# Sharing the scaling of the normed tiles at five layer ends between ScalarE and VectorE

## The chip, the cores and the metric

The kernel runs on one core of a Trainium2 chip. The metric is the device time of one execution in microseconds. Three runs of the kernel before took 980.38, 981.84 and 982.14 us; their median is 981.84 us. The engines are called as the profile calls them: PE (TensorE, matrix products and transposes), DVE (VectorE), ACT (ScalarE), POOL (GpSimd) and SP (SyncE, which issues the loads). Each engine works through its own list of instructions strictly in the order in which they are written, and waits by semaphores for results of the others.

## The reference

The program is a chain of four layers on 256 tokens of width 1024, all in float32: stick-breaking attention with a gated conv feed-forward part, forgetting attention with another feed-forward part, a pooling layer, and a latent (MLA) attention layer. Between any two parts stands the same step: a result is added to the residual stream `h`, `h` is normalised per token, multiplied by a gain vector, and goes into the next projection:

```python
def rmsnorm(x, g):
    xf = x.astype(jnp.float32)
    y = xf * lax.rsqrt(jnp.mean(xf * xf, axis=-1, keepdims=True) + RMS_EPS)
    return (y * g.astype(jnp.float32)).astype(x.dtype)

h = h + rmsnorm(merge_heads(o) @ sb_w_o[layer], sb_post_g[layer])   # an attention's end
f = conv_ffn(rmsnorm(h, ffn_pre_g[layer]), w_up[layer], ...)        # the next part's start
h = h + rmsnorm(f, ffn_post_g[layer])                               # a feed-forward part's end
```

The pooling layer adds its product to `x` without a norm of its own (`return x + y @ w_out`), and the MLA layer then starts with the norm of the sum.

## The kernel before

The 256 tokens are two row tiles of 128, called i = 0 and i = 1 here. Every float32 operand of a product is kept as two float32r parts, a high part (the rounded copy) and a low part (the difference), and each product is three matmuls: high by high, high by low, low by high (lines 79 to 81, and in another order lines 87, 88 and 90). ACT makes high parts (`hi_copy`, line 64) and DVE low parts (`lo_sub`, line 68), of activations and of all weights. Weights stream through a ring: SP loads a chunk of 1 MB into `raw`, and the background steps `bg_hi` and `bg_lo` put one ACT copy and one DVE subtraction of 128x1024 elements (`wh`, `wl`) into the lists of these engines, wherever the code calls them. No scheduler reorders anything: the order of the calls in the code is the order on each engine.

The step between two parts is the function `edge` (line 478). It is called five times: at the end of the first attention (E1), the first feed-forward part (E2), the second attention (E3), the second feed-forward part (E4) and the pooling layer (E5). For row tile 0, `tail0` ends the sums in two PSUM banks (`accO`, `accD` or `accP`; columns 0 to 511 and 512 to 1023, called H0 and H1 here). Then, with `post_add` (E1 to E4):

- `half(n)` takes a bank into the post norm. ACT squares it and sums the squares (`square`, line 383, an ACTIVATE and the reading of its accumulator), and DVE multiplies it by the post gain into `y` (lines 394 and 397). The two read the same bank and never at once: for H0 of row tile 1 DVE goes first and ACT waits for it, for all others ACT goes first.
- `fin` makes the factor r of the post norm on POOL by `rstd_of` (three small operations on 128x1: lines 346, 348 and, with the power, 349) and updates `h` by two DVE operations (line 402).
- `norm_r` sums the squares of `h` on ACT (line 383, two halves), lets DVE make one waiting `wl` (`bg_lo`), and makes the factor of the pre norm on POOL.
- `scaled` (line 370) makes the normed tile `a` = h times r times g, by two DVE operations of 128x512, H0 and then H1.
- `all_T` transposes `a` on PE in two groups of four (`psT`, line 356), and splits each group into the two parts of `aT` by one ACT copy and one DVE subtraction.

With `plain_add` (E5) `half` is a single DVE addition into `h` (line 409) and `fin` is nothing.

`tail1` is PE's last run of matmuls for row tile 1; it stands between the making of r for row tile 0 and the transposes of its `a`, so PE has work while `a` is made. The transposes of row tile 1 come later, from a hook in the next part after its first sums of row tile 0 (`accS` in the feed-forward and pooling parts, `accV` in the second attention, `accL` in MLA). At E2 the code that follows loads another ACT function table (`table_set`, line 115) right behind `edge`.

Of the kernel before, what the change touches and what calls it, by code (L numbers as in the profile page):

```python
# [7 lines left out]
F32 = mybir.dt.float32  # L8
# [3 lines left out]
AF = mybir.ActivationFunctionType  # L12
ALU = mybir.AluOpType
PSUM = bass.MemoryType.PSUM

P = 128
S = 256
NT = S // P
D = 1024
# [17 lines left out]
def tile_net(ctx: ExitStack, tc: tile.TileContext, t, out):  # L37
    nc = tc.nc
    ctx.enter_context(tc.manual_schedule())
    pe, act, dve, pool = nc.tensor, nc.scalar, nc.vector, nc.gpsimd  # L40
# [6 lines left out]
    nat = ctx.enter_context(tc.tile_pool(name="nat", bufs=2))  # L47
# [118 lines left out]
    def bg_hi():  # L166

        n = nxt["hi"]
        if n >= len(parts) or (n >= WBUFS and parts[n - WBUFS]["used"] < parts[n - WBUFS]["need"]):
            return False  # L170
        q = parts[n]
        load_w(q["chunk"])
        k0, k1, c0, c1 = q["cut"]
        for nm, pl_ in (("wh", whp), ("wl", wlp)):
            w = pl_.tile([P, TW], F32R, tag=nm, name=nm)
            q[nm] = w[:, :q["n"]].rearrange("p (a b) -> p a b", a=k1 - k0)
        q["raw"] = loaded[q["chunk"]][:, k0:k1, c0:c1]
        hi_copy(q["wh"], q["raw"], q["scale"] or 1.0)
        nxt["hi"] += 1
        return True  # L180

    def bg_lo():
        while nxt["lo"] < nxt["hi"]:
            n = nxt["lo"]
            q = parts[n]
            lo_sub(q["wl"], q.pop("raw"), q["wh"], q["scale"])
            nxt["lo"] += 1
            if n == specs[q["chunk"]][1][-1]:
                load_w(q["chunk"] + RAWB)
# [111 lines left out]
    h = cst.tile([P, NT, D], F32, name="h")  # L301
# [34 lines left out]
    def mean_sq(srcs, n):  # L336

        ss = sm.tile([P, 2], F32, tag="ss", name="ss")
        for j, x in enumerate(srcs):
            square(x, n, ss[:, j:j + 1])  # L340
        return ss[:, 0:len(srcs)]

    def rstd_of(ss, tag="rstd"):
        r = sm.tile([P, 1], F32, tag=tag, name="rstd")
        s0 = ss[:, 0:1]
        pool.tensor_tensor(out=s0, in0=s0, in1=epsc[:, 0:1], op=ALU.add)  # L346
        if ss.shape[1] == 2:
            pool.tensor_tensor(out=s0, in0=s0, in1=ss[:, 1:2], op=ALU.add)
        pool.tensor_tensor(out=r, in0=s0, in1=epsc[:, 1:2], op=ALU.pow)
        return r  # L350
# [9 lines left out]
    def all_T(src, dst, i):  # L360
        for n in range(2):
            transpose_split(src, dst[n], i, 4 * n)

    HALF = [slice(n * 512, (n + 1) * 512) for n in range(2)]

    def scaled(i, r, g):

        a = nat.tile([P, D], F32, tag="a", name="a")
        for s_ in HALF:
            dve.scalar_tensor_tensor(out=a[:, s_], in0=h[:, i, s_], scalar=r, in1=g[:, s_],  # L370
                                     op0=ALU.mult, op1=ALU.mult)
        return a

    def norm_r(i):

        ss = mean_sq([h[:, i, s_] for s_ in HALF], D)
        bg_lo()
        return rstd_of(ss, "rn")

    def square(x, n, ss):  # L380

# [96 lines left out]
    def edge(tail0, tail1, acc, add, g, dst):  # L478


        tail0()
        half, fin = add(0, acc[0])
        half(0)
        half(1)
        bg_hi()
        fin()
        r0 = norm_r(0)
        tail1()
        half, fin = add(1, acc[1])
        half(0)  # L490
        a0 = scaled(0, r0, g)
        half(1)
        all_T(a0, dst, 0)
        bg_hi()
        fin()
        r1 = norm_r(1)
        return scaled(1, r1, g), (r0, r1)

    def attention(s0, s1, s2, s3, post, w_ids, oT, g_post, dst, hook, late, acc0_tile):

# [91 lines left out]
    for k in (4, 5, 6, 7, 0, 1, 2, 3):  # L592
# [5 lines left out]
    a0 = nat.tile([P, D], F32, tag="a", name="a")  # L598
    y0 = nat.tile([P, D], F32, tag="a", name="y0")
    dve.tensor_tensor_reduce(out=y0[:, HALF[0]], in0=h[:, 0, HALF[1]], in1=h[:, 0, HALF[1]],  # L600
                             scale=1.0 / D, scalar=EPS, op0=ALU.mult, op1=ALU.add,
                             accum_out=ss0[:, 1:2])
    dve.tensor_tensor(out=y0[:, HALF[1]], in0=h[:, 0, HALF[1]], in1=g_ps[1], op=ALU.mult)
    r0 = sm.tile([P, 1], F32, tag="rstd", name="rstd")
# [4 lines left out]
                             op0=ALU.mult, op1=ALU.mult)  # L609
# [6 lines left out]
    r1 = rstd_of(ss1, "rn")  # L616
    a1 = nat.tile([P, D], F32, tag="a", name="a")
    for n, s_ in enumerate(HALF):
        dve.scalar_tensor_tensor(out=a1[:, s_], in0=h[:, 1, s_], scalar=r1, in1=g_ps[n],
                                 op0=ALU.mult, op1=ALU.mult)  # L620
    bg(0)
    with tc.tile_pool(name="sb", bufs=2) as sb, tc.tile_pool(name="sbv", bufs=1) as sbv:
# [97 lines left out]
        with tc.tile_pool(name="ld", bufs=1) as ld:  # L720
            a1 = attention(s0, s1, s2, s3, post, W["sb_o"], oT, g_post, aT2,
                           lambda: load_params(ld), lambda: gain("ffn_pre_g", 0), mm_tile)
# [115 lines left out]
    with tc.tile_pool(name="fxa", bufs=1) as fxa:  # L838
# [3 lines left out]
        a1, rn = ffn(0, aT, a1, lambda: (gain("ffn_post_g", 0), gain("kv_norm_g")), sT)  # L842
# [3 lines left out]
        with tc.tile_pool(name="fx", bufs=2) as fx, tc.tile_pool(name="fxv", bufs=1) as fxv:  # L846
# [27 lines left out]
            for b in (0, 32, 64, 96):  # L874
# [16 lines left out]
                                     op1=ALU.subtract)  # L891
            pool.memset(fe, 1.0)
            dve.tensor_tensor_scan(out=fc, data0=fe, data1=fy, initial=0.0, op0=ALU.mult,
                                   op1=ALU.add)
# [45 lines left out]
            def f3(p):  # L940
# [3 lines left out]
            a1 = attention(f0, f1, f2, f3, lambda p: bg(1), W["fx_o"], oT, g_post, aT,  # L944
                                     gates_T, lambda: gain("ffn_pre_g", 1), acc_tile)

    pT = new_aT()
    a1 = ffn(1, aT, a1, lambda: (gain("ffn_post_g", 1), gain("pool_norm_2", 0)), pT)[0]
# [3 lines left out]
    with tc.tile_pool(name="pl", bufs=2) as pl_, tc.tile_pool(name="plc", bufs=1) as plc:  # L952
# [126 lines left out]
        def lat_mm(x, i, k0, k1):  # L1079
            n, w = lat_w[x]  # L1080
            if k0 == 0:
# [3 lines left out]
                 k0 == 0, k1 == KD)  # L1085

        a1 = edge(lambda: out_rows(acc[0], 0, st["y", 3], wo, k4, False, True, by_half=True),
                  lambda: out_rows(acc[1], 1, st["y", 3], wo, k4, False, True, by_half=True),
                  acc, plain_add, g_pre, mT)[0]
# [411 lines left out]
```

## Time and profile before

| | |
|---|---|
| median of three runs | 981.84 us (980.38 to 982.14) |
| the profiled execution | 981.37 us, its span 979.7 us |
| busy: PE, DVE, ACT, POOL | 965.0, 756.7, 609.7, 71.9 us |
| granted PE clock | 1.00 throughout the five edges |
| idle of PE before transposes that wait for `a` of line 370 | 1.7 us, 3 times |
| the five edges, in us from the span's start | E1 121 to 137, E2 303 to 321, E3 428 to 443, E4 610 to 627, E5 772 to 788 |

A row of the timeline gives the start in us, the duration in us, the engine, the line, the operation, the tile written and the tiles read, their shapes, and the number of instructions that were merged into the row. In brackets stands how long the engine was idle just before, and what it was waiting for. L370 is line 370 of the kernel before; in the changed kernel the lines from 374 on stand nine lines lower.

### The profile page before, as it was taken

Reading aid. Unit: us, or ns where it says so; the run is one execution under the profiler, and the core shown is the slowest. Engines: PE = TensorE matmul, PEld = TensorE weight load, DVE = VectorE, ACT = ScalarE, POOL = GpSimd, SP = SyncE. Lnnn points to the kernel's source line nnn. Section 1 sums busy time; section 2 is a strip of 40 time slices with the busy share of each in tenths; the row PEclk is TensorE's granted clock in tenths of the full one; section 3 lists DMA queues with packets and bytes.
Section 4 is the critical chain, followed back from the end, with each engine's and each line's share of the span. In section 5 each row is a group of like instructions: output and inputs, shape, how many; then the busy total and the mean of one; then the engine's idle time right before and its main releaser. Section 6 shows DMA issues by size and latency. Waiting matters only on the chain.

```text
span 979.7 us, 17580 instructions
## 1 busy us (share of the span) xinstructions
PE 965.0 (99%) x6954; PEld 893.3 (91%) x6954; DVE 756.7 (77%) x1302; ACT 609.7 (62%) x1049; POOL 71.9 (7%) x181
## 2 busy tenths in 40 slices
PE   8999999999999999999999999999999999999997
PEld 6999789999888899889999988899999899999996
DVE  7577788999955969977999973776868677887876
ACT  7499866767744657666676753665434555766563
POOL 1022220000002000020000000200000020110100
PEclk9999999999999999999999999999999999999999
DMA  8724346675572744435666575375555344644521
GB/s 304 241 91 147 130 156 207 198 234 197 179 253 86 230 160 151 157 102 173 202 228 205 183 256 174 100 246 206 175 201 194 110 135 136 212 157 140 163 95 43
DMA packets 116164, 170.27 MB, mean 174 GB/s; under 512 B 4218, under 2 KB 93682, under 8 KB 116082
## 3 DMA queue, kind: packets, MB, share of 16 engines
q1 hardware_dynamic: 116002, 169.15, 51.8%
q8 instruction: 54, 0.88, 0.4%
q14 instruction: 28, 0.23, 0.1%
q0 software_dynamic: 64, 0.00, 0.0%
q10 hardware_dynamic: 16, 0.00, 0.0%
HBM read 168.10 MB, written 1.05 MB: 173 GB/s over the span
## 4 chain that ended last, share of the span: by engine, by line
PE 88%; ACT 5%; DVE 3%; POOL 2%; issue 1%; DMA 1%; SPq 0%; POOLq 0%; DVEq 0%; ACTq 0%
PE psu L79 10%; PE psu L80 10%; PE psu L81 10%; PE accD L81 4%; PE accD L80 4%; PE accD L79 4%; PE psq L79 3%; PE psq L81 3%; PE psq L80 3%; PE accO L79 2%; PE accO L81 2%; PE accO L80 2%; PE accP L79 1%; PE accP L81 1%; PE accP L80 1%; DVE wl L68 1%
## 5 line engine op out<-in xcount | busy, mean ns | idle before, releaser
L68 DVE TENSOR_TENSOR wl<-raw,wh 128x1024 fp32r<-128x1024 f32 (+3 forms) x300 | 352.6, 1197 | 88.5 <-ACT wh L64 85.5
L64 ACT ACTIVATE wh<-raw 128x1024 fp32r<-128x1024 f32 (+3 forms) x316 | 315.4, 1026 | 77.9 <-PE accD L81 30.3
L79 PE MATMUL psu<-aT,wh 128*128 128x256 f32 x864 | 239.5, 277 | 0.0
L80 PE MATMUL psu<-aT,wh 128*128 128x256 f32 x864 | 239.2, 277 | 0.0
L81 PE MATMUL psu<-aT,wl 128*128 128x256 f32 x864 | 239.2, 277 | 0.0
L79 PEld LDWEIGHTS psu<-aT,wh 128*128 128x128 f32 x864 | 162.2, 188 | 0.2
L81 PEld LDWEIGHTS psu<-aT,wl 128*128 128x128 f32 x864 | 162.2, 188 | 0.0
L80 PEld LDWEIGHTS psu<-aT,wh 128*128 128x128 f32 x864 | 162.0, 188 | 0.0
L748 DVE SCALAR_TENSOR_TENSOR yc<-psu,conv,yc 128x255 f32<-128x255 f32 (+1 forms) x160 | 73.5, 480 | 11.6 <-ACT yc L741 8.6
L79 PE MATMUL accD<-wh,gh 128*128 128x512 f32 x176 | 68.7, 390 | 0.0
L81 PE MATMUL accD<-wh,gl 128*128 128x512 f32 x176 | 68.5, 389 | 0.0
L80 PE MATMUL accD<-wl,gh 128*128 128x512 f32 x176 | 68.5, 389 | 0.0
L346 POOL TENSOR_TENSOR ss<-ss,epsc 128x1 f32<-128x1 f32 x23 | 11.6, 506 | 612.3 <-ACT junk L383 612.3
L79 PE MATMUL psq<-aT,wh 128*128 128x256 f32 x192 | 54.0, 281 | 0.1
L80 PE MATMUL psq<-aT,wh 128*128 128x256 f32 x192 | 53.4, 278 | 0.0
L81 PE MATMUL psq<-aT,wl 128*128 128x256 f32 x192 | 53.4, 278 | 0.0
L741 ACT ACTIVATE yc<-psu,conv 128x256 f32<-128x256 f32 x80 | 40.8, 560 | 19.8 <-PE psu L81 19.8
L753 ACT ACTIVATE yc<-yc 128x256 f32<-128x256 f32 x44 | 18.4, 418 | 48.5 <-DVE yc L748 48.5
L64 ACT ACTIVATE qkh<-psq 128x512 fp32r<-128x512 f32 x32 | 19.0, 594 | 33.5 <-PE psq L81 33.3
L80 PEld LDWEIGHTS accD<-wl,gh 128*128 128x128 f32 x176 | 33.1, 188 | 6.8
L79 PEld LDWEIGHTS accD<-wh,gh 128*128 128x128 f32 x176 | 33.0, 188 | 6.8
L81 PEld LDWEIGHTS accD<-wh,gl 128*128 128x128 f32 x176 | 33.0, 188 | 6.8
(347 smaller groups left out, 2272.7 us busy)
## 6 DMA issues: line engine op xcount, KB each, us to landing
raw<-in_w_up_dram SPq DMA_DIRECT2D x44, 1024.0 KB, 5.0
raw<-in_w_down_dram SPq DMA_DIRECT2D x22, 1024.0 KB, 5.9
raw<-in_pool_w_in_dram SPq DMA_DIRECT2D x16, 1024.0 KB, 7.0
raw<-in_sb_w_qkv_dram SPq DMA_DIRECT2D x10, 1024.0 KB, 5.3
raw<-in_w_kvf_dram SPq DMA_DIRECT2D x8, 1024.0 KB, 5.6
raw<-in_pool_w_out_dram SPq DMA_DIRECT2D x8, 1024.0 KB, 5.0
raw<-in_mla_w_in_dram SPq DMA_DIRECT2D x8, 1024.0 KB, 5.3
raw<-in_mla_w_out_dram SPq DMA_DIRECT2D x8, 1024.0 KB, 5.6
```

What stands on the lines that cost most here:

```text
L64: act.activation(out=hi, in_=src, func=AF.Copy, scale=scale)
L68: (eng or dve).tensor_tensor(out=lo, in0=src, in1=hi.bitcast(F32), op=ALU.subtract)
L79: pe.matmul(ps, lhsT=l[0], rhs=r[0], start=first, stop=False)
L80: pe.matmul(ps, lhsT=l[0], rhs=r[1], start=False, stop=False)
L81: pe.matmul(ps, lhsT=l[1], rhs=r[0], start=False, stop=last)
L346: pool.tensor_tensor(out=s0, in0=s0, in1=epsc[:, 0:1], op=ALU.add)
L741: act.activation(out=y[:, u, :], in_=ps[:, u * S:(u + 1) * S], func=AF.Identity, bias=cp[:, 132 + q:133 + q], scale=cp[:, 88 + q:89 + q])
L748: dve.scalar_tensor_tensor(out=y[:, u, d:S], in0=ps[:, u * S:(u + 1) * S - d], scalar=w, in1=y[:, u, d:S], op0=ALU.mult, op1=ALU.add)
L753: act.activation(out=y[:, 0, :], in_=y[:, 0, :], func=AF.Gelu_apprx_tanh)
```

## The change

`norm_r` and the two calls of `scaled` in `edge` are replaced by two functions. `norm_1` does what `norm_r` did, and has DVE put h times g for H1 into the new tile, by a plain product behind the waiting `wl`; it needs no factor r. `norm_2` has ACT multiply this half by r, in place, and DVE make H0 by the same three-operand operation as before. For row tile 0 `norm_2` now stands ahead of `half(0)` of row tile 1; before, `scaled` stood between `half(0)` and `half(1)`. The tile for `a` of row tile 0 is taken from its pool before the tile `y` of row tile 1, and no longer after it. The calls of `bg_hi` and `bg_lo` keep their places among the other calls, and the line that scales for the second attention's own norm still uses `scaled`.

```diff
-    def norm_r(i):
+    def norm_1(i, g):
 
         ss = mean_sq([h[:, i, s_] for s_ in HALF], D)
         bg_lo()
-        return rstd_of(ss, "rn")
+        a = nat.tile([P, D], F32, tag="a", name="a")
+        dve.tensor_tensor(out=a[:, HALF[1]], in0=h[:, i, HALF[1]], in1=g[:, HALF[1]], op=ALU.mult)
+        return a, rstd_of(ss, "rn")
+
+    def norm_2(i, a, r, g):
+
+        act.activation(out=a[:, HALF[1]], in_=a[:, HALF[1]], func=AF.Copy, scale=r)
+        dve.scalar_tensor_tensor(out=a[:, HALF[0]], in0=h[:, i, HALF[0]], scalar=r,
+                                 in1=g[:, HALF[0]], op0=ALU.mult, op1=ALU.mult)
+        return a
...
         half(1)
         bg_hi()
         fin()
-        r0 = norm_r(0)
+        a0, r0 = norm_1(0, g)
         tail1()
         half, fin = add(1, acc[1])
+        norm_2(0, a0, r0, g)
         half(0)
-        a0 = scaled(0, r0, g)
         half(1)
         all_T(a0, dst, 0)
         bg_hi()
         fin()
-        r1 = norm_r(1)
-        return scaled(1, r1, g), (r0, r1)
+        a1, r1 = norm_1(1, g)
+        return norm_2(1, a1, r1, g), (r0, r1)
```

The order of the instructions changes on ACT and DVE. On ACT at E1, between the squares of `h` for row tile 0 and the next weight copy, before:

```order
L383 ACTIVATE junk,ss<-h 128x512 [waits DVE_49,Activation_49] x2
L383 ACTIVATE junk,ss<-accO_1469 128x512 [waits DVE_49,Activation_49]
L383 ACTIVATE junk,ss<-accO_1470 128x512 [waits PE_49,Activation_49]
L64 ACTIVATE aT<-psT 128x4x128 [waits PE_49] x2
L64 ACTIVATE wh<-raw 128x1024
```

and now:

```order
L392 ACTIVATE junk,ss<-h 128x512 [waits DVE_49,Activation_49] x2
L384 ACTIVATE a<-a,rstd 128x512 [waits DVE_49,Pool_49]
L392 ACTIVATE junk,ss<-accO_1469 128x512 [waits DVE_49,Activation_49]
L392 ACTIVATE junk,ss<-accO_1470 128x512 [waits PE_49,Activation_49]
L64 ACTIVATE aT<-psT 128x4x128 [waits PE_49] x2
L64 ACTIVATE wh<-raw 128x1024
```

The scaling of H1 (L384) now stands ahead of the squares of the two banks of row tile 1 (`accO_1469` is its H0, `accO_1470` its H1); the square of H0 waits for DVE in both. On DVE at the same place, from the background `wl` to the low parts of `aT`, before:

```order
L68 TENSOR_TENSOR wl<-raw,wh 128x1024 [waits DMAHW5_49,Activation_49]
L394 TENSOR_TENSOR y<-accO_1469,g 128x512 [waits PE_49]
L370 SCALAR_TENSOR_TENSOR a<-h,rstd,g 128x512 [waits DMAHW2_49,DVE_49,Pool_49]
L370 SCALAR_TENSOR_TENSOR a<-h,rstd,g 128x512
L397 TENSOR_TENSOR y<-accO_1470,g 128x512 [waits Activation_49]
L68 TENSOR_TENSOR aT<-psT,aT 128x4x128 [waits Activation_49] x2
```

and now:

```order
L68 TENSOR_TENSOR wl<-raw,wh 128x1024 [waits DMAHW5_49,Activation_49]
L379 TENSOR_TENSOR a<-h,g 128x512 [waits DMAHW2_49,DVE_49]
L385 SCALAR_TENSOR_TENSOR a<-h,rstd,g 128x512 [waits Pool_49]
L403 TENSOR_TENSOR y<-accO_1469,g 128x512 [waits PE_49]
L406 TENSOR_TENSOR y<-accO_1470,g 128x512 [waits Activation_49]
L68 TENSOR_TENSOR aT<-psT,aT 128x4x128 [waits Activation_49] x2
```

The product for `y` of H0 (L394, now L403) stood ahead of the operation that waits for POOL's factor and now stands behind it. On ACT at the end of E2, from the square of H1 of row tile 1 to the first high part of the second attention's values, before:

```order
L383 ACTIVATE junk,ss<-accD_3286 128x512 [waits PE_49,Activation_49]
L64 ACTIVATE aT<-psT 128x4x128 [waits PE_49] x2
L64 ACTIVATE wh<-raw 128x1024
L383 ACTIVATE junk,ss<-h 128x512 [waits DVE_49,Activation_49] x2
L115 ACT_TABLE_LOAD
L64 ACTIVATE aT<-psT 128x4x128 [waits PE_49] x2
L64 ACTIVATE vh<-accV 128x512
```

and now:

```order
L392 ACTIVATE junk,ss<-accD_3288 128x512 [waits PE_49,Activation_49]
L64 ACTIVATE aT<-psT 128x4x128 [waits PE_49] x2
L64 ACTIVATE wh<-raw 128x1024
L392 ACTIVATE junk,ss<-h 128x512 [waits DVE_49,Activation_49] x2
L384 ACTIVATE a<-a,rstd 128x512 [waits DVE_49,Pool_49]
L115 ACT_TABLE_LOAD
L64 ACTIVATE aT<-psT 128x4x128 [waits PE_49] x2
L64 ACTIVATE vh<-accV 128x512
```

The scaling of row tile 1's H1, which waits for POOL's factor, now stands ahead of the table load.

## The prediction, made before the changed kernel ran

> **What bounds the kernel now.** I read the page first, then the waits of PE, then the timelines of the five edges with all engines.
>
> ```profile
> PE 965.0 (99%) x6954; PEld 893.3 (91%) x6954; DVE 756.7 (77%) x1302; ACT 609.7 (62%) x1049; POOL 71.9 (7%) x181
> ...
> PE psT L356 <- DVE a L370: 1.7, 3, 0.8
> ```
>
> PE is busy for all but 14.7 of 979.7 us, and its longest wait in total is on `a`, 1.7 us. So the most that the change can give back is small, and whatever it adds between the end of `tail1` and PE's next matmul is added to the time in full. The span is 979.7 us, the execution 981.37 (1.67 around it), and the median of the runs is 0.47 above that. The sums below are made against 981.37.
>
> At E1, for row tile 0, engine by engine:
>
> ```profile
> 125.11 1.22 DVE L68 TENSOR_TENSOR wl<-raw,wh 128x1024 fp32r<-128x1024 f32 x1
> 126.24 0.69 DVE L394 TENSOR_TENSOR y<-accO,g 128x512 f32<-128x512 f32 x1
> 127.31 1.42 DVE L370 SCALAR_TENSOR_TENSOR a<-h,rstd,g 128x512 f32<-128x512 f32 x2 [0.39 <-POOL rstd L349]
> ...
> 127.02 0.60 ACT L383 ACTIVATE junk<-accO 128x512 bf16<-128x512 f32 x1 [0.92 <-DVE y L394]
> ...
> 127.74 0.60 ACT L383 ACTIVATE junk<-accO 128x512 bf16<-128x512 f32 x1
> ...
> 128.88 1.26 ACT L64 ACTIVATE aT<-psT 128x512 fp32r<-128x512 f32 x2 [0.45 <-PE psT L356]
> ...
> 125.42 0.95 POOL L346 TENSOR_TENSOR ss<-ss,epsc 128x1 f32<-128x1 f32 x1 [1.69 <-ACT junk L383]
> 126.45 0.19 POOL L348 TENSOR_TENSOR ss<-ss 128x1 f32<-128x1 f32 x1
> 126.72 0.55 POOL L349 TENSOR_TENSOR rstd<-ss,epsc 128x1 f32<-128x1 f32 x1
> 127.79 0.32 POOL L346 TENSOR_TENSOR ss<-ss,epsc 128x1 f32<-128x1 f32 x1 [0.51 <-ACT junk L383]
> ...
> 128.21 1.29 PE L356 MATMUL psT<-ident,a 128*128 128x128 f32 x8 [0.76 <-DVE a L370]
> ...
> 129.52 0.19 PEld L87 LDWEIGHTS accS<-wh,aT 128*128 128x128 f32 x1 [0.26 <-ACT aT L64]
> 129.53 0.38 PE L87 MATMUL accS<-wh,aT 128*128 128x256 f32 x1
> ```
>
> What the reader is to see: POOL's factor r is there at 127.27. Both squares of row tile 1 run on ACT while PE waits for `a`, and ACT is idle again for 0.45 us before its first copy of `aT`. PE then goes on 0.65 us after that copy began (128.88 to 129.53); it is this copy of H0 that releases it, and not the second group of transposes. Before the first square ACT waited 0.92 us for `y`, and it started 0.09 us after `y` was done (126.93). The two squares start 0.72 us apart.
>
> **The change part by part.** Ten DVE operations of line 370 become ten plain products. Ten ACT operations are new. Their durations are bounded by like rows elsewhere, a scaling of 128x512 by a factor from POOL (its r at 5.81, so it starts 0.09 later) and a `wl` of this size:
>
> ```profile
> 5.90 0.72 ACT L607 ACTIVATE a<-y,rstd 128x512 f32<-128x512 f32 x1 [1.68 <-POOL rstd L606]
> ...
> 7.33 0.69 DVE L68 TENSOR_TENSOR wl<-raw,wh 128x512 fp32r<-128x512 f32 x1 [0.74 <-ACT wh L64]
> ```
>
> The plain product costs the same as the `y` whose place it takes (0.69), and H1 is ready at about the same moment as H0, some 0.7 us sooner than before. That is the gain, and at E1 it is worth nothing: the second group of transposes was not what PE waited for.
>
> *The order, E1 and E3.* `y` of H0 now stands behind the operation that waits for r. With r as before, that starts at 127.31, `y` one step later (1.42 / 2 = 0.71) at 128.02, and ends at 128.71. The first square follows at 128.80, the second at 129.52. Both stand ahead of the copies of `aT` in ACT's list. The rows of E2 below give 0.59 us from the start of the second square to the first copy (311.83 to 312.42): 130.11 for 128.88. PE goes on at 130.76 for 129.53: **1.23 us** lost. Behind ACT and PE, everything of row tile 1 comes as much later. E3 has the same rows (the wait of 0.92 there too):
>
> ```profile
> 433.62 0.60 ACT L383 ACTIVATE junk<-accO 128x512 bf16<-128x512 f32 x1 [0.92 <-DVE y L394]
> ...
> 433.91 1.41 DVE L370 SCALAR_TENSOR_TENSOR a<-h,rstd,g 128x512 f32<-128x512 f32 x2 [0.39 <-POOL rstd L349]
> ```
>
> *POOL against DVE.* POOL's L346 took 0.95 us at 125.42 and ended at 126.37, when DVE's `wl` ended (126.33); the same operation needs 0.19 (L348 beside it). At 127.79 it took 0.32 and ended at 128.11, when the first of two L370 ended (128.05), though the second followed directly. Beside `y`, with an input in PSUM, L348 took its 0.19. So a DVE operation with both inputs in SBUF shuts POOL out until its end, and POOL gets its turn before the next. The new product `h` times `g` has both inputs in SBUF and runs from 126.24 to 126.93, over L348's place: L348 would end at 126.97 for 126.64, r is **0.33 us** later. If the product does not hold POOL, it is 0; if POOL doesn't get its turn in between, L346 ends at 126.97, and r comes at 127.87, 0.60 later. I take 0.33, for which the row at 127.79 speaks. The Trainium skill says it as a rule (SBUF — State Buffer, Who interferes with whom): a VectorE instruction with two SBUF inputs contends with a GpSimd instruction that reads SBUF, whoever starts first keeps the port for its whole length, and the other is blocked. It speaks against this change; by it the 0 falls away, and by the rows alone it stays as a bound.
>
> *Row tile 1, E1.*
>
> ```profile
> 132.10 1.22 DVE L68 TENSOR_TENSOR wl<-raw,wh 128x1024 fp32r<-128x1024 f32 x1
> 132.41 0.95 POOL L346 TENSOR_TENSOR ss<-ss,epsc 128x1 f32<-128x1 f32 x1 [3.01 <-ACT junk L383]
> 133.44 0.19 POOL L348 TENSOR_TENSOR ss<-ss 128x1 f32<-128x1 f32 x1
> ...
> 134.30 1.42 DVE L370 SCALAR_TENSOR_TENSOR a<-h,rstd,g 128x512 f32<-128x512 f32 x2 [0.98 <-POOL rstd L349]
> ...
> 135.11 1.32 PE L356 MATMUL psT<-ident,a 128*128 128x128 f32 x8
> ...
> 136.45 0.39 PE L87 MATMUL accS<-wh,aT 128*128 128x256 f32 x1
> ```
>
> Again `wl`, then the new product, then r: another 0.33. PE had no slack here (0.81 us from the start of `a` to the transposes), so its L87 at 136.45 moves by 1.23 + 0.33 + 0.33 = **1.89 us**, and the same at E3: 3.78 together. (PE's 5.58 us of matmuls between 129.53 and 135.11 would end at 136.7 and do not bind; `a` comes at 137.0.)
>
> *E2 and E4.*
>
> ```profile
> 310.03 1.41 DVE L370 SCALAR_TENSOR_TENSOR a<-h,rstd,g 128x512 f32<-128x512 f32 x2 [0.97 <-POOL rstd L349]
> ...
> 311.83 0.60 ACT L383 ACTIVATE junk<-accD 128x512 bf16<-128x512 f32 x1 [1.97 <-PE accD L81]
> ...
> 312.42 1.08 ACT L64 ACTIVATE aT<-psT 128x512 fp32r<-128x512 f32 x2
> ...
> 316.69 1.28 ACT L115 ACT_TABLE_LOAD   x1
> ...
> 317.30 0.55 POOL L349 TENSOR_TENSOR rstd<-ss,epsc 128x1 f32<-128x1 f32 x1
> ...
> 319.44 0.60 ACT L64 ACTIVATE aT<-psT 128x512 fp32r<-128x512 f32 x1 [1.47 <-PE psT L356]
> ...
> 320.09 0.50 PE L87 MATMUL accV<-wh,aT 128*128 128x512 f32 x1
> ...
> 616.98 1.41 DVE L370 SCALAR_TENSOR_TENSOR a<-h,rstd,g 128x512 f32<-128x512 f32 x2 [1.25 <-POOL rstd L349]
> ...
> 618.50 0.60 ACT L383 ACTIVATE junk<-accD 128x512 bf16<-128x512 f32 x1 [1.75 <-PE accD L81]
> ```
>
> `tail1` is longer, r is ready before its end, and no `wl` waits here for row tile 0, so the port costs nothing at first. `y` starts at 310.03 + 0.71, ends at 311.43, the squares begin at 311.52 and 312.24: 0.41 us after the 311.83 that PE allowed. At E4: 616.98 + 0.71 + 0.69 + 0.09 + 0.72 = 619.19 for 618.50, 0.69. For row tile 1 the port adds 0.33: E4 is **1.02 us**. At E2 the table load stood in a gap of ACT and cost nothing; now the scaling, which waits for r, is ahead of it. r came at 317.85; plus 0.41, 0.33 and 0.09 the scaling starts at 318.68, ends at 319.40, the load ends at 320.68, and the copy that began at 319.44 begins then: with 0.65 more PE goes on at 321.35 for 320.09, **1.26 us**. The row below shows an ACTIVATE 0.02 us after a load (151.62 after 151.60). The Trainium skill (ScalarE: Activation LUTs, What ACT_TABLE_LOAD costs) adds about 1.38 us of drain to each switch; this trace has none of it behind the load, so the row decides; by the page E2 would be 2.6.
>
> ```profile
> 150.32 1.28 ACT L753 ACT_TABLE_LOAD   x1 [1.53 <-DVE yc L748]
> 151.62 0.42 ACT L753 ACTIVATE yc<-yc 128x256 f32<-128x256 f32 x1
> ```
>
> *E5.* `half` has no square, so the order costs nothing. Row tile 1's scaling holds up a weight copy:
>
> ```profile
> 784.17 1.55 DVE L370 SCALAR_TENSOR_TENSOR a<-h,rstd,g 128x512 f32<-128x512 f32 x2 [1.30 <-POOL rstd L349]
> 785.65 1.15 DVE L68 TENSOR_TENSOR wl<-raw,wh 128x960 fp32r<-128x960 f32 x1
> ...
> 782.95 0.99 ACT L64 ACTIVATE wh<-raw 128x960 fp32r<-128x960 f32 x1
> ...
> 786.96 0.31 PE L88 MATMUL accL<-wl,aT 128*128 128x320 f32 x1
> ```
>
> The scaling runs from 784.24 to 784.96, the copy to 785.95, `wl` from 786.04 to 787.19, and PE's L88 takes it at 787.25 for 786.96: **0.3 us**.
>
> Sum: 3.78 + 1.26 + 1.02 + 0.3 = 6.36 us, so 981.37 + 6.36 = 987.7, or 988.2 from the median. I say **988.0**. Between the edges PE is full, so nothing gives it back.
>
> **The rivals.** *POOL is not held by the product.* Then E1 and E3 are 1.23 each, E2 0.93, E4 0.69, E5 0.3: 4.38, so 985.8. The y row beside L348 shows that not every DVE operation holds POOL; against it stands that `wl` has the same form as the product. *POOL is shut out across both DVE operations.* r is 0.60 later each time: E1 and E3 1.23 + 1.20 = 2.43, E2 1.53, E4 1.29, E5 0.3: 7.98, so 989.4. The row at 127.79 is against it. *The time is not longer:* PE's wait on `a` is what counts, and H1 from ACT halves it; 1.7 / 2 = 0.9, so 980.5. For it speaks that this is PE's longest wait. It needs ACT through with both squares when the first transposes are done, at 128.88 in E1; the sum has them end at 130.1, so the rows are against it. It could be so only if `y` did not wait behind r.
>
> **How the numbers follow.** The forecast 0.55, POOL free 0.24, POOL shut out longer 0.13, not longer 0.08. The range reaches 1 us below the second case and 0.6 above the third, for the run-to-run spread and mis-sized steps: 984.8 to 990.0. A change of 0.2% (2 us) is what a measurement of this kernel can tell from none. The first three cases are all slower by more (0.91 after 0.01 for what they miss); of the last I give 0.03 to faster and 0.06 to the same.
>
> **What would show it.** At E1, ACT's first copy of `aT` directly behind the second square of `accO`, with no wait for `psT`, at about 1.5 us later; the same at E3. L348 of POOL at 0.4 to 0.5 us beside the product. The table load after the scaling, and PE waiting for ACT at its first `accV` behind it. L88 waiting for `wl` at E5. I am wrong if ACT still waits for `psT` at E1, or if PE's idle time at the edges grows by less than 4 us or more than 8.

## The result, and the profile after

The changed kernel took 987.83 us (median of five runs, 987.5 to 992.9) against 981.84 us (980.38 to 982.29, five runs) for the kernel before on the same chip: a ratio of 1.0071, with a 95% interval of 1.0052 to 1.009. It is slower by 6.0 us, where 6.4 was the sum.

The profiled execution of the changed kernel is the longest of its five, 992.9 us with a span of 991.2. What sets it apart from the other four is a stretch of 100 us far from the edges, in which PE worked at another pace; it is shown under the last experiment. The same program was profiled once more as the first experiment, at 987.84 us, and the sizes below are taken from there. The waits of PE, in the first profile of the changed kernel (total in us, times, longest):

```profile
PE accS L87 <- ACT aT L64: 4.4, 6, 1.4
PE psT L356 <- DVE a L385: 2.4, 3, 1.1
```

Before, PE's longest wait was for `a`, 1.7 us in total; that has grown to 2.4, and another, 0.5 us before, stands above it: PE waits 4.4 us for ACT's copies into `aT`. The edge E1 shows how, engine by engine (DVE, ACT, POOL, PE; the places that were shown of before):

```profile
126.32 0.69 DVE L379 TENSOR_TENSOR a<-h,g 128x512 f32<-128x512 f32 x1
127.72 0.75 DVE L385 SCALAR_TENSOR_TENSOR a<-h,rstd,g 128x512 f32<-128x512 f32 x1 [0.72 <-POOL rstd L349]
128.39 0.68 DVE L403 TENSOR_TENSOR y<-accO,g 128x512 f32<-128x512 f32 x1
...
127.72 0.72 ACT L384 ACTIVATE a<-a,rstd 128x512 f32<-128x512 f32 x1 [1.54 <-POOL rstd L349]
129.17 0.60 ACT L392 ACTIVATE junk<-accO 128x512 bf16<-128x512 f32 x1 [0.72 <-DVE y L403]
...
129.89 0.60 ACT L392 ACTIVATE junk<-accO 128x512 bf16<-128x512 f32 x1
...
130.47 1.07 ACT L64 ACTIVATE aT<-psT 128x512 fp32r<-128x512 f32 x2
...
125.50 0.95 POOL L346 TENSOR_TENSOR ss<-ss,epsc 128x1 f32<-128x1 f32 x1 [1.68 <-ACT junk L392]
126.53 0.53 POOL L348 TENSOR_TENSOR ss<-ss 128x1 f32<-128x1 f32 x1
...
128.62 1.06 PE L356 MATMUL psT<-ident,a 128*128 128x128 f32 x8 [1.10 <-DVE a L385]
131.11 0.58 PE L87 MATMUL accS<-wh,aT 128*128 128x256 f32 x1 [1.43 <-ACT aT L64]
```

L348 takes 0.53 us beside the new product (0.19 before), so r is late. `y` (L403) stands behind the operation that waits for r; ACT idles 0.72 us for it, makes both squares, and only then, without any idle time, the first copy of `aT` at 130.47. PE idles 1.10 us for `a` (0.76 before) and then 1.43 us for that copy, where before only the weight load of L87 waited for it, 0.26 us. H1 by ACT is there at 128.44, and nothing waits for it.

At E2 the table load is where it was expected, behind ACT's scaling, and the copy that PE waits for is behind the load (ACT and PE, first profile of the changed kernel):

```profile
321.73 0.72 ACT L384 ACTIVATE a<-a,rstd 128x512 f32<-128x512 f32 x1 [1.54 <-POOL rstd L349]
322.47 1.28 ACT L115 ACT_TABLE_LOAD   x1
323.76 1.09 ACT L64 ACTIVATE aT<-psT 128x512 fp32r<-128x512 f32 x2
...
324.41 0.50 PE L87 MATMUL accV<-wh,aT 128*128 128x512 f32 x1 [0.72 <-ACT aT L64]
```

The copy starts 0.01 us after the end of the load (322.47 + 1.28 = 323.75).

### The profile page after: what moved, and what is told of

It reads as the page before. It is cut to its first block, busy times and chain, and to the rows that moved or that the text cites. A ratio compares the mean times of both kernels' runs of the same rounds, so it can differ in the third digit from the quotient of the medians.

```text
span 991.2 us, 17588 instructions
## 1 busy us (share of the span) xinstructions
PE 971.0 (98%) x6954; PEld 901.3 (91%) x6954; DVE 754.6 (76%) x1302; ACT 616.0 (62%) x1059; POOL 73.8 (7%) x181
## 4 chain that ended last, share of the span: by engine, by line
PE 84%; ACT 7%; DVE 4%; POOL 3%; issue 1%; DMA 1%; POOLq 0%; SPq 0%; DVEq 0%; ACTq 0%
PE psu L81 10%; PE psu L80 10%; PE psu L79 10%; PE accD L80 4%; PE accD L81 4%; PE accD L79 4%; PE psq L79 3%; PE psq L81 3%; PE psq L80 3%; PE accO L79 2%; PE accO L81 2%; PE accO L80 2%; PE accP L79 1%; PE accP L81 1%; PE accP L80 1%; ACT junk L392 1%
## 5 line engine op out<-in xcount | busy, mean ns | idle before, releaser
L346 POOL TENSOR_TENSOR ss<-ss,epsc 128x1 f32<-128x1 f32 x23 | 11.6, 505 | 625.4 <-ACT junk L392 625.4
```

## The experiments

All times are medians beside runs of the kernel before on the same chip. "Delay of PE" is the start of a matmul in one profile less the start of the same matmul in the profile of before (both kernels issue the same 6954 in the same order); by how much it grows across an edge is what the edge costs.

### The changed kernel once more

No edit.

> The changed kernel once more, for a profile without the slow stretch of its first one (there PE ran 4% slower from 455 to 570 us at a granted clock of 1.00, which cost 4.4 us, and the granted clock was 0.63 from 130 to 134 us). Theory (order of y and port of POOL): 986.5 to 988.5, L348 of POOL again 0.53 us beside the product, ACT's first copy of aT at E1 about 1.5 us later than before, steps of PE's shift of about 1.9 us at E1 and E3, 1.1 at E2, 0.7 at E4 where the clock is 1.00 throughout. Rival (the slow clock and the slow stretch are most of the loss): an undisturbed execution is below 984.

Measured: 987.69 us (985.29 to 988.98), a ratio of 1.0064 (1.0050 to 1.0078) to 981.41. DVE and PE at E1:

```profile
124.03 1.42 DVE L411 SCALAR_TENSOR_TENSOR h<-y,rstd,h 128x512 f32<-128x512 f32 x2 [0.26 <-POOL rstd L349]
...
131.29 0.39 PE L87 MATMUL accS<-wh,aT 128*128 128x256 f32 x1 [1.43 <-ACT aT L64]
...
138.60 0.39 PE L87 MATMUL accS<-wh,aT 128*128 128x256 f32 x1 [0.25 <-ACT aT L64]
```

In the profile of before the two L87 stand at 129.53 and 136.45. The differences, 1.76 and 2.15, less the 0.25 by which the update of `h` ahead of them is late already (123.78 there), are 1.51 and 1.90: the sum had 1.56 and 1.89. The delays by edge, all from this profile:

| | row tile 0, expected | measured | row tile 1, expected | measured |
|---|---|---|---|---|
| E1 | 1.56 | 1.52 | 0.33 | 0.37 |
| E2 | 0.41 | 0.37 | 0.85 | 0.81 |
| E3 | 1.56 | 1.51 | 0.33 | 1.3 |
| E4 | 0.69 | 0.37 | 0.33 | 0.34 |
| E5 | 0 | 0 | 0.3 | 0.2 |

The measured columns add up to 6.8 us; 0.2 us stands ahead of E1, 0.5 us is given back between 339 and 353 us of the kernel before, away from any edge, and the profile (987.84 less 981.37) is 6.5 longer. Two places are off: E3's row tile 1, 1.0 us too much, and E4's row tile 0, 0.3 too little. E3 has to do with the clock (below). At E5 the cause is the one that was forecast: the weight copy stands behind ACT's scaling, DVE's `wl` waits 0.90 us for it, and PE's L88 starts at 793.30, 0.05 us after the end of `wl`. The 0.5 us are PE's pace (shown under the last experiment): the 119 intervals between matmuls in that stretch are 117.7 ns long in the profile of before and 113.4 here.

### The order put back

```diff
-        norm_2(0, a0, r0, g)
         half(0)
+        norm_2(0, a0, r0, g)
         half(1)
```

> The scaling of row tile 0 put behind half(0) again, so y stands ahead of the operation that waits for r; all else as changed. Theory: at E1 and E3 row tile 0 loses only what the scaling on ACT, now between the two squares, adds (0.7 us where it lost 1.2 without the port), nothing at E2 and E4; the port's 0.33 per waiting product stays. Worked out: E1 and E3 1.0 each, E2 0.85, E4 0.33, E5 0.3, so 3.5 us over the kernel before, 985.3. Rival (the order is not what counts, ACT's added work or the port is): 987 to 988.5, as the changed kernel.

Measured: 984.29 us (982.29 to 985.12), a ratio of 1.0030 (1.0018 to 1.0041). The delays of PE are 0.53 and 0.38 at E1, 0.81 at E2, 0.54 and 0.37 at E3, 0.34 at E4 and 0.2 at E5, 3.2 in all, where 3.5 was worked out. ACT, POOL and PE at E1:

```profile
128.24 0.60 ACT L392 ACTIVATE junk<-accO 128x512 bf16<-128x512 f32 x1 [1.52 <-DVE y L403]
128.82 0.71 ACT L384 ACTIVATE a<-a,rstd 128x512 f32<-128x512 f32 x1
130.01 1.08 ACT L64 ACTIVATE aT<-psT 128x512 fp32r<-128x512 f32 x2
...
127.07 0.53 POOL L348 TENSOR_TENSOR ss<-ss 128x1 f32<-128x1 f32 x1
...
130.65 0.39 PE L87 MATMUL accS<-wh,aT 128*128 128x256 f32 x1 [0.41 <-ACT aT L64]
```

`y` goes ahead of r again, the first square starts as soon as `y` is done, and PE's wait for the copy falls from 1.43 to 0.41 us. The order alone is worth 3.4 us (987.69 less 984.29; 3.6 by PE's delays, 0.9 of which are E3's low clock, gone with the long wait: the mean clock is 0.998 or 0.999 in all seven runs, as in the kernel before). What is left, 2.9 us over the kernel before, is made of POOL's L348 at 0.53 us, unchanged by this edit, of 0.2 us each at E1 and E3, where the scaling now stands between the two squares, of the table load at E2, which still stands behind the scaling (0.48 us without POOL's part, by the next experiment), and of E5's 0.2.

### The product left out

```diff
-        dve.tensor_tensor(out=a[:, HALF[1]], in0=h[:, i, HALF[1]], in1=g[:, HALF[1]], op=ALU.mult)
...
-        act.activation(out=a[:, HALF[1]], in_=a[:, HALF[1]], func=AF.Copy, scale=r)
+        act.activation(out=a[:, HALF[1]], in_=h[:, i, HALF[1]], func=AF.Copy, scale=r)
```

> The product h times g for H1 is left out, and ACT scales h itself, so H1 of the five normed tiles lacks the gain. DVE's order is as changed but for the ten products. Theory (the product shuts POOL out): L348 takes 0.19 us again at E1, r is 0.33 us earlier for both row tiles at E1 and E3 and for row tile 1 at E2 and E4, together 2.0 us, so 985.9. Rival (POOL's delay is hidden or has another cause): L348 stays near 0.5 us, or the time stays at 987 to 988.5.

Measured: 986.07 us (984.33 to 986.35), a ratio of 1.0047 (1.0034 to 1.0059). POOL and PE at E1:

```profile
126.65 0.20 POOL L348 TENSOR_TENSOR ss<-ss 128x1 f32<-128x1 f32 x1
...
130.91 0.39 PE L87 MATMUL accS<-wh,aT 128*128 128x256 f32 x1 [1.43 <-ACT aT L64]
```

L348 is back at 0.20 us, while PE's wait for the copy stays at 1.43. PE's delays are 1.2 and 0.05 at E1, 0.37 and 0.48 at E2, 1.21 and 0 at E3, 0.38 and 0 at E4, 0.2 at E5. So the product costs nothing that shows by its own duration, and 1.6 us (987.69 less 986.07; 2.0 by PE's delays, E3's low clock left aside) by what it does to POOL. The two causes are apart: taking one away leaves the other's rows as they were.

### PE's idle time filled

```diff
-        for j in range(m):
+        for j in [*range(m)] * (1 + again):
...
-            transpose_split(src, dst[n], i, 4 * n)
+            transpose_split(src, dst[n], i, 4 * n, again=n * again)
...
-        all_T(a0, dst, 0)
+        all_T(a0, dst, 0, again=2 if add is not plain_add else 0)
```

> The changed kernel with the second group of transposes of row tile 0 done three times at E1 to E4 (eight transposes more, 1.0 us, while PE would wait for ACT). If the low granted clock at E1 and E3 is an answer to PE's idle time there, PE being busy takes it away: the granted clock of 130 to 134 us is 1.00, each place where it fell is about 1.4 us shorter, of which about 0.4 come back as a longer wait for row tile 1, so up to 2 us less than the changed kernel, 986 to 987. If the clock has nothing to do with the idle time, the time is that of the changed kernel, 987 to 988.5, and the low clock stays.

Measured: 987.59 us (985.44 to 989.14), a ratio of 1.0062 (1.0048 to 1.0076). The gain of up to 2 us did not show in the time. The clock did change. PE at E1, where eight transposes have become 16:

```profile
128.81 1.94 PE L356 MATMUL psT<-ident,a 128*128 128x128 f32 x16 [1.11 <-DVE a L385]
...
131.31 0.39 PE L87 MATMUL accS<-wh,aT 128*128 128x256 f32 x1 [0.56 <-ACT aT L64]
```

PE idles 0.56 us for the copy instead of 1.43 and goes on at the same moment. The windows behind E1 and E3 in the first profile of the changed kernel (from:to in us, length, then busy time and count of PE, PEld, DVE, ACT and POOL, the granted clock, the DMA share and GB/s):

```profile
131.10:134.60 3.50, 3.49 (x17) 3.49 (x18) 3.50 (x6) 2.72 (x6) 0.99 (x2) 0.53 0.02 7
441.80:445.20 3.40, 3.40 (x19) 3.40 (x18) 3.40 (x6) 2.45 (x6) 0.89 (x2) 0.52 0.00 0
```

the same in the profile of the repeat:

```profile
130.00:134.00 4.00, 2.71 (x23) 2.71 (x24) 3.21 (x6) 3.22 (x8) 0.94 (x3) 1.00 0.02 6
440.30:443.80 3.50, 3.38 (x17) 3.38 (x18) 3.50 (x6) 2.72 (x6) 0.99 (x2) 0.54 0.00 1
```

and here, with the idle time filled, behind E3:

```profile
437.00:444.00 7.00, 5.45 (x45) 5.24 (x46) 5.37 (x8) 5.36 (x12) 1.57 (x5) 1.00 0.43 147
```

PE was granted half its clock for 3.41 us right after its wait for the copy, at both edges in one profile and at E3 alone in the other. That is E3's extra microsecond in the table: the matmuls of row tile 0 came 1.4 us later, which hides a part of the wait for row tile 1. With the fill it was granted full clock there. The mean clock of an execution is 0.998 or 0.999 in all runs of the kernel before; it is so in five of six runs with the fill, and in two of eleven of the changed kernel (0.995 to 0.997 in the other nine). So the low clock is shown to come of the idle time that the change opens. That it costs time is shown by PE's delay at E3 in one profile (1.3 for 0.38), but not by the medians, whose runs differ by more than that.

### Only row tile 1 shared

```diff
-        r1 = norm_r(1)
-        return scaled(1, r1, g), (r0, r1)
+        a1, r1 = norm_1(1, g)
+        return norm_2(1, a1, r1, g), (r0, r1)
```

(a diff against the kernel before, with the two new functions.)

> Only row tile 1 shares its scaling; row tile 0 is scaled as before. By the measured steps (delay of PE against the kernel before, in the runs above) row tile 1 costs 0.37 us at E1, 0.8 at E2, 0.37 at E3, 0.34 at E4 and 0.2 at E5 when it stands alone: 2.1 us, so about 983.5. At row tile 0 PE should stand where it stood before, to 0.1 us. Rival 1, the cost of row tile 1 is only there because row tile 0 came late: then it is hidden here, and the time is that of the kernel before, 981.4. Rival 2, H1 from ACT gives the transposes of row tile 1 an earlier end that shows once row tile 0 is not delayed: below 981.

Measured: 983.3 us (981.22 to 987.78, twelve runs) against 981.34, a ratio of 1.0016 (0.9993 to 1.0039). The time alone does not part it from no change; PE's delays do: 0 at row tile 0 of E1 and E3, and 0.33, 0.82, 0.36, 0.16 and 0.2 at row tile 1 of E1 to E5, 1.9 in all (E4 is less than elsewhere because the sum of row tile 0 ahead of it went at the slower of the two paces shown below, which hides 0.2 us). The rivals fall: the cost of row tile 1 is there without row tile 0's, and H1 from ACT gains nothing. POOL and PE at E1, row tile 1:

```profile
133.59 0.53 POOL L348 TENSOR_TENSOR ss<-ss 128x1 f32<-128x1 f32 x1
...
136.93 0.39 PE L87 MATMUL accS<-wh,aT 128*128 128x256 f32 x1 [0.25 <-ACT aT L64]
```

### Without the weight splits inside the edges

The L346 of 0.95 us is a cost of the kernel before: the subtraction `wl` stands over it. If that could stand elsewhere, r would come sooner in both kernels. Three kernels tried it.

```diff
-        bg_lo()
         return rstd_of(ss, "rn")
...
         half(1)
-        bg_hi()
         fin()
...
         all_T(a0, dst, 0)
-        bg_hi()
         fin()
```

> The kernel before (no sharing), without the background weight splits inside the edges (one ACT copy and one DVE subtraction each); the next background steps elsewhere make them. Port theory: the subtraction has both inputs in SBUF and shuts POOL out just where POOL makes the factor, so without it L346 of POOL takes 0.2 to 0.3 us for 0.95, r comes 0.26 us sooner at E1 and E3 for row tile 0 (then the second square's end at 126.11 bounds it), and PE waits less for a; with row tile 1 some 1.0 us less in all: about 980.4. Rival, the splits are needed where they stand: weights come late, PE waits for wl or wh somewhere behind an edge, and the time is 982 or more.

The second is the same with H0 in two operations:

```diff
-        for s_ in HALF:
+        for s_ in (slice(0, 256), slice(256, 512), HALF[1]):
             dve.scalar_tensor_tensor(out=a[:, s_], in0=h[:, i, s_], scalar=r, in1=g[:, s_],
```

> As the one before, and H0 of the normed tile is made in two DVE operations of 256 columns, so that the first two transposes can start after half of H0. If PE's wait for a counts by its first operation alone, another 0.2 us each at E1 and E3 and at the row tiles where PE waits for a: 980.0 or a little less. Rival: PE's resumption is set by the copy of the four transposes of H0, whose last needs all of H0, and one more operation costs DVE 0.06 us or more: the same time as the one before, or 0.2 to 0.4 more.

The third is the changed kernel with the order put back, and without the splits:

```diff
-        norm_2(0, a0, r0, g)
         half(0)
+        norm_2(0, a0, r0, g)
...
-        bg_lo()
...
-        bg_hi()
```

> The changed kernel with norm_2 of row tile 0 behind half(0) of row tile 1 (as in e1_order), and without the background weight splits inside the edges (as in e5_no_background): the sharing with both of its costs taken away. The product then stands where the subtraction stood, and is over at 125.8 us, before the second square of h is summed at 126.11, so POOL is not held. Theory: the earlier H1 is worth nothing to PE even then; the time is that of e5_no_background or a little above (ACT's scaling stands between the two squares and may put the first copy of aT 0.1 to 0.2 us later): 980.4 to 981.2. Rival, H1 from ACT is worth something once it costs nothing: 0.3 us or more below e5_no_background. If POOL is held by the product at row tile 1 even so: 981.5 to 983.

Measured: 1009.89, 1008.95 and 1009.28 us, ratios of 1.0271 (1.0228 to 1.0313), 1.0278 (1.0239 to 1.0317) and 1.0281 (1.0242 to 1.0320). The expected times were missed by some 29 us in all three, and the rival that was named, late weights, is the case. PE's waits over the whole of the first of them, and two rows of its PE:

```profile
PE accS L88 <- DVE wl L68: 7.8, 3, 3.4
PE accS L87 <- ACT wh L64: 1.8, 2, 1.6
...
134.03 0.38 PE L87 MATMUL accS<-wh,aT 128*128 128x256 f32 x1 [1.56 <-ACT wh L64]
...
136.64 0.58 PE L88 MATMUL accS<-wl,aT 128*128 128x256 f32 x1 [2.22 <-DVE wl L68]
```

The last two rows are PE behind E1: the `wl` that the kernel before makes at 125.11 is read some 6 us after its end, and without those calls the next one makes it, behind the work of row tile 1. In all PE waits 22.7 us in that profile, for 7.7 before, and it was granted half its clock for 20.5 us behind such waits. Whether an earlier place would do was not tried.

Up to that wait the three profiles still answer what they were built for. The time from the start of the last matmul of `tail1` to the start of PE's first L87 at E1 is read from two rows each. Kernel before:

```profile
127.07 0.39 PE L81 MATMUL accO<-wh,oTl 128*128 128x512 f32 x1
```

(and its L87 at 129.53: 2.46 us). Without the splits, POOL and PE:

```profile
125.58 0.19 POOL L346 TENSOR_TENSOR ss<-ss,epsc 128x1 f32<-128x1 f32 x1 [1.68 <-ACT junk L382]
...
127.23 0.39 PE L81 MATMUL accO<-wh,oTl 128*128 128x512 f32 x1
...
129.47 0.39 PE L87 MATMUL accS<-wh,aT 128*128 128x256 f32 x1
```

With H0 in two operations as well:

```profile
127.35 0.39 PE L81 MATMUL accO<-wh,oTl 128*128 128x512 f32 x1
...
129.45 0.38 PE L87 MATMUL accS<-wh,aT 128*128 128x256 f32 x1
```

With the sharing, order put back and no splits, POOL and PE:

```profile
126.28 0.19 POOL L348 TENSOR_TENSOR ss<-ss 128x1 f32<-128x1 f32 x1 [0.27 <-ACT junk L391]
...
127.11 0.39 PE L81 MATMUL accO<-wh,oTl 128*128 128x512 f32 x1
...
129.35 0.39 PE L87 MATMUL accS<-wh,aT 128*128 128x256 f32 x1 [0.25 <-ACT aT L64]
```

That is 2.24, 2.10 and 2.24 us. Without the subtraction beside it, L346 takes 0.19 us for 0.95, and PE goes on 0.22 us sooner. And the sharing, with both of its costs out of the way (L348 at 0.19, `y` ahead of r), brings PE back exactly as soon as no sharing does. An earlier H1 is worth nothing at E1, even when it costs nothing.

### H0 in two operations, and the subtraction in four

The first is the kernel before with the edit to `scaled` shown above, the second has the following edit besides.

> The kernel before with one edit: H0 of the normed tile is made in two DVE operations of 256 columns instead of one of 512 (H1 as before); the background splits stay. Without the background splits the same edit let PE's first matmul of accS stand 0.14 us closer behind the end of tail1 at E1 (2.10 us for 2.24). If that holds here at the row tiles where PE waits for a (both at E1 and E3, row tile 1 at E2 and E4), PE is 0.6 to 0.8 us earlier at the end: 980.6, which the time alone can hardly tell from 981.3. Rival: the 0.13 us that the added operation costs DVE reaches r of row tile 1 (its y stands behind): the gain of row tile 0 is given back at row tile 1, and PE stands where it stood before.

> As the one before, and the background subtraction in front of the pre norm's factor is made in four DVE operations of 128x256 instead of one of 128x1024. If POOL gets its turn between two DVE operations, L346, which took 0.95 us under the one of 1.22 us, takes 0.4 us or less, and r comes 0.1 to 0.25 us sooner at row tile 0 of E1 and E3 and at row tile 1 of all: another 0.4 to 1.0 us, 979.8 to 980.3. Rival, POOL stays shut out as long as DVE has such operations without a gap: L346 stays at 0.95 us or more, r is 0.1 to 0.2 us later since the four take longer than the one, and the time is 981.5 to 982.5.

```diff
-    def bg_lo():
+    def bg_lo(m=1):
...
+            for j in range(m):
+                k_ = slice(j * ka // m, (j + 1) * ka // m)
+                lo_sub(q["wl"][:, k_], raw[:, k_], q["wh"][:, k_], q["scale"])
...
-        bg_lo()
+        bg_lo(4)
         return rstd_of(ss, "rn")
```

Measured: 990.71 us (984.29 to 991.02) and 986.44 us (979.37 to 989.95) against 981.05, ratios of 1.0077 (1.0056 to 1.0098) and 1.0053 (1.0036 to 1.0070). Neither was expected. At the edges the first does what the rival said: at E3 PE's delay falls by 0.15 us at row tile 0 and grows by 0.13 at row tile 1. In the second POOL (row tile 1 of E1) shows what the four operations are for:

```profile
132.91 0.49 POOL L350 TENSOR_TENSOR ss<-ss,epsc 128x1 f32<-128x1 f32 x1 [2.88 <-ACT junk L387]
133.73 0.34 POOL L352 TENSOR_TENSOR ss<-ss 128x1 f32<-128x1 f32 x1 [0.33 <-ACT junk L387]
```

L350 (L346 before) takes 0.49 us where it took 0.95: POOL gets its turn between two DVE operations that follow each other directly. The next sum waits for ACT's second square of `h` and then takes 0.34 us for 0.19 beside the last of the four, so r gains next to nothing, and PE's delays at the edges are as in the first. All that both kernels lost, they lost elsewhere.

### Where they lost it: the pace of PE

A window of the second feed-forward part in which PE does nothing but `psu`, with full clock granted (from:to, length, then busy time and count of PE, PEld, DVE and ACT on that tile, the clock, the DMA share and GB/s). Kernel before:

```profile
500.00:540.00 40.00, 40.00 (x355) 40.00 (x354) 13.64 (x30) 7.16 (x14) 1.00 0.68 226
```

H0 in two operations at both row tiles:

```profile
500.00:540.00 40.00, 40.00 (x342) 40.00 (x341) 13.26 (x30) 7.15 (x14) 1.00 0.65 216
```

The same matmuls, with PE never idle, at 342 for 355. From start to start they are 117.8 ns apart for 113.3, and there is nothing between the two values: each of the stretches of 959 such intervals, in every profile, is at one of them from its first to its last, a difference of 4.3 us. Two more kernels made the edit at one row tile each.

```diff
-        for s_ in HALF:
+        for s_ in ((slice(0, 256), slice(256, 512)) if i == 0 else (HALF[0],)) + (HALF[1],):
```

(and `i == 1` in the other.)

> As e8_quarters, at row tile 0 alone. The question is the pace of PE: in the profile of e8_quarters the 256-column matmuls of psu start 117.8 ns apart all through both feed-forward parts, in that of the kernel before 113.3 ns, and this made 8.7 of its 9.3 us; the slow pace began right behind the transposes of row tile 1. If the way PE restarts at row tile 1 (two short waits instead of one) sets the pace of the stage behind it, this kernel keeps 113.3 ns and takes about the time of before, 980.8 to 981.5. Rival, the pace goes with any change in the build or by chance: slow stages here too, 985 to 990.

> As e8_quarters, at row tile 1 alone. If PE's restart at row tile 1 sets the pace, both feed-forward parts go at 117.8 ns in most runs: 988 to 991. Rival: 113.3 ns in the feed-forward parts and 981 to 982.

Measured: 982.04 us (981.04 to 985.96, twelve runs), a ratio of 1.0001 (0.9982 to 1.0020), and 990.21 us (985.05 to 991.98, ten runs), 1.0059 (1.0030 to 1.0087), against 981.51. Row tile 0 alone:

```profile
500.00:540.00 40.00, 40.00 (x355) 40.00 (x355) 13.76 (x31) 7.16 (x14) 1.00 0.68 227
```

Row tile 1 alone:

```profile
500.00:540.00 40.00, 40.00 (x342) 40.00 (x341) 13.25 (x30) 7.15 (x14) 1.00 0.65 215
```

So it is with the edit at row tile 1 that most runs lose some 9 us, though it moves no more than a few tenths at the edge itself. The pace of a feed-forward part is that with which PE takes up the sum `accS` behind the transposes of row tile 1: in all 14 profiles, with two such parts each, both were the same in all 28 cases. It is not carried over from the sum of row tile 0 just before: in seven of the 22 cases outside the three kernels without splits the two differ. What in that restart sets the pace stays open. The edit moves the odds rather than deciding alone: at E1 of the last kernel already the sum of row tile 0, which the edit doesn't touch, went at the second pace; without the splits, the kernel with H0 in two operations has the first pace in both parts, and the one with H0 whole has the second in one; and the kernel before has runs of 985 to 991 us too (four of 21 beside these two kernels, four of 17 beside the kernels without splits, none of 17 beside the two of the section before). Those were only timed, so the pace in them is inferred from their times.

Other stretches have the two paces as well, and not only behind transposes: the one between 339 and 353 us, which gave 0.5 us back in the repeat, begins directly behind matmuls of 512 columns. In the pooling layer 479 intervals are 117.8 ns long in the kernel before and 113.3 in the profile with the order put back, which is 2.1 us; so the time of that one profile (982.29) does not show the 3.2 us that its edges cost.

For the result this matters once. The first profile of the changed kernel shows

```profile
500.00:540.00 40.00, 40.00 (x342) 40.00 (x341) 12.85 (x28) 7.15 (x14) 1.00 0.63 211
```

in the second feed-forward part, and its repeat 355 there. That is most of the 5 us between 992.9 us and the median. Between before (981.37) and the repeat (987.84) the paces are the same in both feed-forward parts, and the 6.5 us are what the edges cost, with E3's low clock, less the 0.5 us given back.

## Why the prediction was right, point by point

*The order at E1 and E3.* The step of 1.23 us, with 0.33 for POOL, made 1.56 for row tile 0; 1.52 and 1.51 were measured, and each row behind it (the wait of 0.72 for `y`, two squares 0.72 apart, the copy with no wait for `psT`) is where the sum had it. Putting the order back took away 3.4 us.

*POOL against DVE.* 0.33 us was taken from bounds of 0 and 0.60: L348 took 0.53 for 0.19, and row tile 1 came 0.37 and 0.34 us later where nothing else interfered. Both bounds are excluded, the 0 by the kernel without the product (L348 back at 0.20), the 0.60 by the changed kernel's own rows at E1: L346 ends at 126.45, 0.05 us behind the `wl` that stood over it, and L348 starts at 126.53, though the product follows `wl` directly. In the medians it is 1.6 us where the steps gave 2.0.

*E2.* 0.41 and 0.85 were expected, 0.37 and 0.81 measured; the load started 0.02 us after the scaling, and the copy 0.01 after the load.

*E4, row tile 0: the step of 0.69 us was too large, 0.37 was measured.* It was worked out from the `a` at 616.98, and that was late in this one execution. The squares of row tile 0 just ahead, in the kernel before:

```profile
608.97 0.60 ACT L383 ACTIVATE junk<-accD 128x512 bf16<-128x512 f32 x1 [3.08 <-PE accD L81]
...
611.97 0.60 ACT L383 ACTIVATE junk<-accD 128x512 bf16<-128x512 f32 x1 [2.31 <-PE accD L81]
```

and in the repeat of the changed kernel:

```profile
614.47 0.60 ACT L392 ACTIVATE junk<-accD 128x512 bf16<-128x512 f32 x1 [3.02 <-PE accD L81]
...
617.25 0.60 ACT L392 ACTIVATE junk<-accD 128x512 bf16<-128x512 f32 x1 [2.09 <-PE accD L81]
```

They are 3.00 us apart there and 2.78 here; the delays are 5.50 and 5.28, while PE's own was 5.56 at this place. So r, which comes of these squares, stood 0.28 us nearer to PE's work in the repeat, and 0.69 less 0.28 is 0.41, as at E2. The place is like E2 in every step, and the unlike row (616.98) should have been a warning.

*E5.* 0.3 expected, 0.2 measured, by the mechanism that was forecast.

*The sign by PE's idle time.* PE's waits for `a` and for the copies of `aT` (the lines 356, and 87 into `accS` and `accV`) are 2.9 us in the profile of before and 8.9 in the repeat: 6.0 more, between the 4 and 8 that were named.

*"Between the edges PE is full, so nothing gives it back."* This sentence failed, in both directions. 0.5 us was given back between 339 and 353 us, and at E3 1.0 us more was lost than the sum had. Neither was in it: the pace of a full PE is not fixed, nor is its clock behind a gap at an edge. The sum of 6.36 stands beside a measured 6.5 (one profile) and 6.0 and 6.3 (medians) partly because these two and E4's 0.3 cancel: that part of the agreement is luck.

*The rivals.* POOL free (985.8) is excluded by L348; POOL shut out for longer by row tile 1's 0.37; a time that is not longer by every edge. The wait for `a`, on which the last rested, did not halve but grew, and the experiments without the splits show why it could not pay: H1 is not what PE waits for.

## What to carry to other kernels

Before an operation is split between two engines, ask which half the next engine waits for: here the consumer restarted on the first half, so that an earlier second half was worth nothing, while each edit made for it had its price. In strictly ordered lists an operation that waits for a factor must stay behind the ones that do not (3.4 us for one swapped line), and a DVE operation with both inputs in SBUF must not stand over a short POOL operation on the critical path (1.6 us); if it has to stand there, several short ones let POOL in sooner than one long one. And a change of some microseconds is to be read at the matmuls around the edit, in profiles whose paces agree, since PE's pace alone moved this kernel by 4 to 9 us.

## What the hardware showed that was not expected

*Two paces.* Back-to-back matmuls of 128x256 start 113.3 or 117.8 ns apart at full granted clock, for whole stages; a restart behind transposes can change it. With one edit at row tile 1 both feed-forward parts of the profiled execution went at the second, for 9 us.

*The clock.* PE was granted half its clock for 3.41 us after waits of 1.1 and 1.43 us with eight transposes between them: from the end of `tail1` to the next sum (127.52 to 131.11 in the rows of E1) 3.6 us with nothing else, for 2.1 in the kernel before (127.46 to 129.53). The Trainium skill (TensorE: Matmul & The Clock Gate, Part 1: The HAM clock gate) has a free-running window of about 3.4 us, and half clock after at least one idle window; the length agrees, and that the drop came at E1 in one profile and not in the other fits a window that runs free. That PE has to be idle for the whole window is not what these traces show. Within a profile all low stretches start on one grid of 3.413 us, and what goes with them is PE's busy share, by the profile, of the window of that grid just before:

| window, us from the span's start | PE busy | of which transposes | clock after it |
|---|---|---|---|
| changed kernel, first profile, E1: 127.60 to 131.01 | 0.31 | 0.31 | half |
| changed kernel, first profile, E3: 438.21 to 441.62 | 0.37 | 0.31 | half |
| its repeat, E1: 126.07 to 129.48 and 129.48 to 132.90 | 0.67 and 0.58 | 0.20 and 0.11 | full |
| its repeat, E3: 436.68 to 440.10 | 0.35 | 0.31 | half |
| order put back, E1: 127.18 to 130.60 | 0.57 | 0.32 | full |
| H0 in two operations, no splits, behind E3: 447.41 to 450.83 | 0.52 | 0 | half |

In the repeat the grid happened to cut the gap at E1 in two. Over the 14 profiles, from 60 us to shortly before the end, each of the 16 windows at full clock that were 0.52 busy or less was followed by half clock, and none of the others was, of which the least busy was at 0.54. Transposes count as work here: without them the window of the kernel with the order put back would be 0.25 busy, and the clock stayed full. That fits the idle time filled: with 16 transposes for eight the least busy window at its edges is at 0.67.

*POOL's turn.* Under one DVE operation of 1.22 us a POOL operation on 128x1 took 0.95 us, under four of a quarter each 0.49, and with none beside it 0.19.
